# Attention with three score regions in one five-bank PSUM tile, one batch of products per group, and ScalarE's copy of turned weights ahead of the next exponential

## The chip, the core and the metric

The kernel runs on one NeuronCore of a Trainium2 chip. Its time is the device time of one launch in microseconds (us). Five engines take part, each with an instruction queue of its own that is worked through in order: TensorE (PE in the profile, with its weight loads as PEld), VectorE (DVE), ScalarE (ACT), GpSimd (POOL) and SyncE (SP, which issues transfers). They meet through semaphores. Products land in PSUM, a memory of eight banks of 512 fp32 columns on 128 partitions.

## What is computed

The reference is two transformer layers and a hybrid block (gated linear attention, an mLSTM memory and a state-space layer, then a feed-forward net). The change touches only the two attentions of the transformer layers: 512 latent and 256 context tokens of width 1024, 16 heads each. The first has 4 heads to one key/value head (GQA), and the context rows attend too; in the second each head has keys and values of its own (MLA), and only the latent rows attend.

```python
def block_attention(q, k, v):          # swept over blocks of 128 queries
    ...
    def one_block(qi):
        s = jnp.einsum('bqhgd,bkhd->bhgqk', qi, k, preferred_element_type=jnp.float32) * scale
        p = jax.nn.softmax(s, axis=-1).astype(v.dtype)
        return jnp.einsum('bhgqk,bkhe->bqhge', p, v)
```

## The kernel before, in words

Both attentions run through one routine, `attend`. Its work is a list of units. A unit is one head's 128 queries against all 768 keys (in the first attention also, for the context rows, two heads' 128 queries against 256 keys). Four heads' units, or two such pairs, make a group whose outputs are written together. The GQA attention has 64 long units in 16 groups and then 16 short units in 8 groups. The MLA attention has 64 units, four for each of 16 heads; stages of its own (projections of keys, values and queries, their rotation, and the casts of a head pair) are woven between the units at given positions.

What happens to a unit:

- `scores` (L716, MLA L1013): TensorE multiplies queries with keys into a PSUM tile `s` of 128x768 fp32. Queries and keys are split into high and low parts, so GQA has two and MLA three products for each of the two column pieces (512 and 256, a product may not cross a bank).
- the row maximum (L603, VectorE reads `s`), and `bias` (L680, MLA L997), which makes the exponent's offset from it.
- `exps` (L631, ScalarE reads `s`, writes the weights `p` to SBUF and sums them; the read of the sum is a small instruction of its own).
- `softmax_end`: the sum's reciprocal (L637, VectorE) and the scaling of `p` (L640, GpSimd).
- `turn`, LAG = 4 units later: six transposes of `p` on TensorE (L660; L653 in short units) into tiles `pt`, four in the first and two in the second, copied to SBUF as `pT` by ScalarE and VectorE (L661, L655).
- `products`, when a group's four units are turned: TensorE multiplies `pT` with the values into a PSUM tile `ob` (L722, MLA L1021), 12 products for a long group (the trace shows each as two rows). `high` casts `ob` to fp32r on ScalarE (L734, MLA L1034) and `low` takes the remainder on VectorE (L738, MLA L1040); both run in a later pass through the loop.
- `prepare`, once a group: transposes of the next queries (`tq`, L698) and their split (L702, L703, L706, L707).

Inside `manual_schedule` each engine's instructions stand in the order in which the code issues them: nothing reorders them, and the framework only adds the semaphore waits that the tiles' uses call for. So the body of the loop over `n` is the order of each queue. In one pass it issues the pending `high`s, the exponential of unit n-1, `turn` of unit n-4, the scores of unit n with their maximum and bias, `softmax_end` of unit n-1, the pending `low`s, a stage if one is due, and a few of the group's products: `per` keys, 2 in long GQA groups, 1 in short ones, 3 in MLA. A group's products are thus spread over two or three passes.

PSUM before: two tiles `s` of 1024 columns (two banks each, `pss` with bufs=2), and a pool `psp` of four tiles of one bank, from which `pt`, `tq`, the stages' `st` and `ob` are taken in turn.

Of the kernel before, what the change touches and what calls it, by code (L numbers as in the profile page):

```python
# [9 lines left out]
F32 = mybir.dt.float32  # L10
# [6 lines left out]
PSUM = bass.MemoryType.PSUM  # L17
P = 128
# [8 lines left out]
class Bump:  # L27


    def __init__(self, *regions):  # L30
        self.free = list(regions)
        self.tags = {}
# [273 lines left out]
class GqaNet(Base):  # L306
# [103 lines left out]
    def gqa(self):  # L410
        nc, i, tc, flow = self.nc, self.i, self.tc, self.flow
        W = i["gqa_w_qkv"][0]
        with ExitStack() as ph:
# [6 lines left out]
            with tc.tile_pool(name="q0", bufs=1, reuse_waits="tile") as pool, tc.tile_pool(name="q0ps", bufs=2, reuse_waits="tile", space=PSUM) as ps:  # L420
# [46 lines left out]
                b = self.turn_cols(rows, ps, pool, "b")  # L467
# [52 lines left out]
                            flow.add(ada.pop(0))  # L520
                flow.finish()
                self.ada_bufs = 2
            with tc.tile_pool(name="a0", bufs=1, reuse_waits="tile") as pool, tc.tile_pool(name="a0s", bufs=2, reuse_waits="tile", space=PSUM) as pss, \
                    tc.tile_pool(name="a0p", bufs=4, reuse_waits="tile", space=PSUM) as psp:
                units = []
                for ts in (range(4), (4, 5)):
                    for o in range(2):
                        for t in ts:
                            for g in (2 * o, 2 * o + 1):
                                gr = GqaGroup(self, pool, Q, K, V, t, g)  # L530
                                units += [(gr, (x,)) for x in range(4)] if t < 4 else [(gr, (0, 1)), (gr, (2, 3))]
                stages = {}
                none = lambda: None
                for n, (gr, xs) in enumerate(units):
                    if xs[0] == 0:
                        stages.setdefault(n - 3, []).append(gr.prepare(psp))
                n = 8
                for t in range(6):
                    for f in self.q_rope(None, Q, t, 1):
                        stages.setdefault(n, []).append((f, none, none))  # L540
                        n += 2
                ada = self.ada_steps(0, 11, pool, psp, None, True)
                next(ada)
                for x in range(2):
                    stages.setdefault(1 + x, []).insert(0, (lambda: next(ada, None), none, none))
                self.ahead = []
                for x in range(2):
                    for y, f in enumerate(self.out_weights(i["gqa_w_o"][0], x)):
                        stages.setdefault(n - 2 + 6 * x + 2 * y, []).append((f, none, none))
                self.attend(units, pool, pss, psp, stages)  # L550
# [18 lines left out]
    def attend(self, units, pool, pss, psp, stages):  # L569

        nc = self.nc
        N = len(units)
        work, highs, lows = [], [], []
        for n in sorted(k for k in stages if k < 0):
            for fs in stages[n]:
                for f in fs:
                    f()
        with self.tc.manual_schedule():  # L580
            for n in range(N + LAG + 6):
                for f in highs:
                    f()
                highs, late, lows = [], lows, []
                if 1 <= n <= N:
                    self.exps(pool, *units[n - 1])
                if LAG < n <= N + LAG and units[n - LAG - 1][0].last == units[n - LAG - 1][1][-1]:
                    g, xs = units[n - LAG - 1]
                    g.ob = psp.tile([P, 2, 128], F32, name="ob", tag="pt")
                    work.append((g, g.products()))  # L590
                if LAG <= n < N + LAG:
                    g, xs = units[n - LAG]
                    self.turn(pool, psp, g, xs)
                if n < N:
                    g, xs = units[n]
                    s = pss.tile([P, 1024], F32, name="s", tag="s")
                    m = self.sp.tile([P, 3, 2], F32, name="sm", tag="sm", bufs=6)
                    for k, x in enumerate(xs):
                        g.scores(x, s[:, k * g.nk:(k + 1) * g.nk])
                    if n == 0:  # L600

                        nc.scalar.activation(self.sp.tile([P, 1], F32, name="se", tag="se", bufs=1), s[:, :1], AF.Exp, scale=0.0)
                    nc.vector.tensor_reduce(out=m[:, 0, :len(xs)], in_=s[:, :g.nk * len(xs)]  # L603
                                            .rearrange("p (k n) -> p k n", k=len(xs)), axis=AX.X, op=ALU.max)
                    g.sm[xs] = s, m
                    g.bias(xs, m)
                if 1 <= n <= N:
                    self.softmax_end(*units[n - 1])
                for f in late:
                    f()  # L610
                for pe, high, low in stages.get(n, []):
                    pe()
                    highs.append(high)
                    lows.append(low)
                if work:
                    g, fs = work[0]
                    for f in fs[:g.per]:
                        f()
                    del fs[:g.per]
                    if not fs:  # L620
                        work.pop(0)
                        highs.append(g.high)
                        lows.append(g.low)
            assert not work and not highs and not lows

    def exps(self, pool, g, xs):
# [37 lines left out]
class GqaGroup:  # L664


    def __init__(self, net, pool, Q, K, V, t, g):
        self.net, self.pool, self.Q, self.K, self.V, self.t, self.g = net, pool, Q[t], K, V, t, g
        self.c0, self.nk = (0, NL + NC) if t < 4 else (NL, NC)
        self.keys = list(range(6)) if t < 4 else [4, 5]  # L670
        self.p, self.sm, self.last = {}, {}, 3
        self.per = 2 if t < 4 else 1

    def scale(self, x):
        return self.net.RS[:, self.t, 4 * self.g + x:4 * self.g + x + 1]
# [32 lines left out]

        return turn, high, low

    def scores(self, x, s):
        q = self.q[x % 2][:, 128 * (x // 2):128 * (x // 2) + 128]
        for j in range(2):
            for n0 in range(0, self.nk, 512):
                n1 = min(self.nk, n0 + 512)
                self.net.nc.tensor.matmul(s[:, n0:n1], lhsT=q, rhs=self.K[j][:, self.g, self.c0 + n0:self.c0 + n1],  # L716
                                          start=j == 0, stop=j == 1)

# [265 lines left out]
class MlaHead:  # L984

    last = 3
    per = 3

    def __init__(self, m, h):
        self.m, self.net, self.h, self.nk = m, m.net, h, NL + NC  # L990
# [13 lines left out]
            self.pT.append(pool.tile([P, 6, 2, 128], F32, name="pT", tag="pT", bufs=3))  # L1004
        return self.pT[x // 2][:, :, x % 2, :]

    def scores(self, x, s):
        e = self.h % 2
        (qh, ql), (kh, kl) = self.m.Q[e], self.m.K[e]
        c = slice(128 * x, 128 * x + 128)  # L1010
        for k, (a, b) in enumerate(((qh, kh), (qh, kl), (ql, kh))):
            for n0, n1 in ((0, 512), (512, 768)):
                self.net.nc.tensor.matmul(s[:, n0:n1], lhsT=a[:, c], rhs=b[:, n0:n1], start=k == 0, stop=k == 2)  # L1013

    def products(self):
# [32 lines left out]
class MlaNet(MlpNet):  # L1048
    def mla(self):
        nc, i, tc = self.nc, self.i, self.tc  # L1050
        m = Mla(self)
        self.m = m
        with ExitStack() as ph:
            mp = ph.enter_context(tc.tile_pool(name="mp", bufs=1, reuse_waits="tile"))
            tcf = [T.rearrange("p a b -> p (a b)") for T in self.TC]
            xf = self.XN.rearrange("p a b -> p (a b)")
            m.cqT = [mp.tile([P, 3, NL], F32R, name=f"cqT{j}") for j in range(2)]
            m.ckT = [t[:, :1536].rearrange("p (k n) -> p k n", k=2) for t in tcf]
            m.qpe = xf[:, :2048].rearrange("p (t h f) -> p t h f", t=4, h=16)


            kk = mp.tile([P, 2, 2, NL + NC], F32R, name="K")
            m.K = [[kk[:, e, j, :] for j in range(2)] for e in range(2)]
            m.Q = [[tcf[j][:, 1536:] for j in range(2)], [mp.tile([P, NL], F32R, name=f"Q1{j}") for j in range(2)]]
            with tc.tile_pool(name="mA", bufs=1, reuse_waits="tile") as pool:
                self.mla_in(pool, m, kk.rearrange("p e j n -> p (e j n)"))
            self.l0.close()
            with tc.tile_pool(name="a1", bufs=1, reuse_waits="tile") as pool, tc.tile_pool(name="a1s", bufs=2, reuse_waits="tile", space=PSUM) as pss, \
                    tc.tile_pool(name="a1p", bufs=4, reuse_waits="tile", space=PSUM) as psp:
                self.mla_attend(pool, pss, psp, m.cqT, m.ckT, m.qpe, m)  # L1070

    def row_rs(self, pool, x, n):
# [1625 lines left out]
```

## Time and profile before

| | |
|---|---|
| median of 3 runs | 2687.36 us (2685.77 to 2690.11) |
| the profiled execution's own time | 2689.55 us |
| its span | 2687.7 us |
| GQA attention, long units | 158.9 to 310.5 us of the span |
| GQA attention, short units | 310.5 to 348.3 us |
| MLA attention, 64 units | 1064.8 to 1292.4 us |

The page of the profile gives each engine's busy time over the span. The views of the trace used below are: a table of stretches (busy time of each engine in each), the waits (which instruction waited for which, summed), and the timeline (single instructions in order of time; "idle before" in brackets, with what ended it). Times of the timeline count from the span's start.

### The profile page before, as it was taken

What the parts mean: (1) busy time and instruction counts of PE and PEld (TensorE: products, weight loads), DVE (VectorE), ACT (ScalarE), POOL (GpSimd) and SP (SyncE); (2) the same over time, 40 slices, a digit from 0 to 9 for tenths busy, and PEclk for the clock granted to TensorE, in tenths of its full rate; (3) what the DMA queues carried; (4) which work ended last, traced back from release to release, by engine and by line L of the source; (5) the groups of instructions that cost most, each with busy time, mean ns of one, the idle gap of its engine ahead of it and who ended that gap; (6) DMA issues with size and microseconds to landing.
All of it is one profiled execution on the core that took longest, in us unless ns stands there. A gap on an engine that the chain in (4) does not pass through costs nothing. (4 is left out here: it accounts for less than half of the span.)

```text
span 2687.7 us, 37906 instructions
## 1 busy us (share of the span) xinstructions
PE 2588.1 (96%) x14954; PEld 2118.7 (79%) x14954; DVE 1734.3 (65%) x3102; ACT 1156.9 (43%) x2016; POOL 649.7 (24%) x541
## 2 busy tenths in 40 slices
PE   8999999999999999999999899989999999999998
PEld 5666689888888898777787678877678888888887
DVE  4458847876666577788488987576675533534445
ACT  4357835333333235655364344253563223532222
POOL 0224322233322013333134445043140011000000
PEclk9999999999999999999999999999999999999999
DMA  8510221333333112000255454234123234222221
GB/s 317 205 32 1 66 92 34 124 120 126 118 122 101 62 39 69 19 33 17 64 166 172 138 174 158 95 107 117 46 68 102 86 94 137 75 94 94 94 94 63
DMA packets 178644, 264.83 MB, mean 99 GB/s; under 512 B 18019, under 2 KB 116954, under 8 KB 177954
## 3 DMA queue, kind: packets, MB, share of 16 engines
q1 hardware_dynamic: 173010, 257.89, 29.0%
q10 hardware_dynamic: 5456, 4.51, 0.6%
q8 instruction: 118, 1.93, 0.3%
q14 instruction: 60, 0.49, 0.1%
HBM read 256.81 MB, written 5.58 MB: 98 GB/s over the span
## 5 line engine op out<-in xcount | busy, mean ns | idle before, releaser
L129 DVE TENSOR_TENSOR wl<-raw,wh 128x1024 fp32r<-128x1024 f32 (+1 forms) x301 | 397.7, 1334 | 358.8 <-ACT wh L126 355.9
L126 ACT CAST wh<-raw 128x1024 fp32r<-128x1024 f32 (+1 forms) x301 | 306.7, 1034 | 618.8 <-PE mm L140 449.7
L139 PE MATMUL mm<-TL,wh 128*128 128x512 f32 (+2 forms) x1512 | 565.7, 375 | 6.1 <-ACT TL L387 4.7
L140 PE MATMUL mm<-TL,wh 128*128 128x512 f32 (+2 forms) x1512 | 561.5, 372 | 4.5 <-DVE TL L388 4.4
L141 PE MATMUL mm<-TL,wl 128*128 128x512 f32 (+2 forms) x1512 | 560.1, 371 | 0.0
L139 PEld LDWEIGHTS mm<-TL,wh 128*128 128x128 f32 (+1 forms) x1512 | 287.2, 190 | 60.5 <-ACT TL L387 5.6
L140 PEld LDWEIGHTS mm<-TL,wh 128*128 128x128 f32 (+1 forms) x1512 | 287.7, 190 | 54.8 <-DVE TL L388 6.0
L141 PEld LDWEIGHTS mm<-TL,wl 128*128 128x128 f32 (+1 forms) x1512 | 287.3, 190 | 52.5
L139 PE MATMUL mm<-TC,wh 128*128 128x256 f32 (+1 forms) x672 | 223.6, 333 | 7.8 <-ACT low L867 7.8
L640 POOL TENSOR_SCALAR p<-p,sm 128x768 f32<-128x768 f32 (+1 forms) x160 | 156.1, 978 | 297.0 <-DVE sm L637 201.9
L141 PE MATMUL mm<-TC,wl 128*128 128x256 f32 (+1 forms) x672 | 223.0, 332 | 0.0
L140 PE MATMUL mm<-TC,wh 128*128 128x256 f32 (+1 forms) x672 | 222.8, 332 | 0.0
L258 POOL TENSOR_TENSOR XN<-XN 128x512 f32<-128x512 f32 x84 | 132.4, 1594 | 282.4 <-ACT XN L251 279.6
L139 PE MATMUL mm<-gh,wh 128*128 128x256 f32 (+1 forms) x544 | 179.7, 330 | 0.3 <-DVE RL L878 0.3
L140 PE MATMUL mm<-gl,wh 128*128 128x256 f32 (+1 forms) x544 | 178.7, 329 | 0.0
L141 PE MATMUL mm<-gh,wl 128*128 128x256 f32 (+1 forms) x544 | 178.1, 328 | 0.0
L258 POOL TENSOR_TENSOR low<-low 128x512 f32<-128x512 f32 x84 | 136.0, 1632 | 152.9 <-ACT low L251 150.1
L603 DVE TENSOR_REDUCE sm<-s 128x1 f32<-128x768 f32 (+1 forms) x144 | 132.7, 922 | 22.5 <-PE s L1013 11.4
L139 PEld LDWEIGHTS mm<-TC,wh 128*128 128x128 f32 x672 | 127.5, 190 | 23.3 <-ACT low L867 9.1
L140 PEld LDWEIGHTS mm<-TC,wh 128*128 128x128 f32 x672 | 127.6, 190 | 13.9
L141 PEld LDWEIGHTS mm<-TC,wl 128*128 128x128 f32 x672 | 127.6, 190 | 12.7
L660 PE MATMUL pt<-ident,p 128*128 128x128 f32 x768 | 116.0, 281 | 17.5 <-ACT pT L661 7.8
(614 smaller groups left out, 4978.8 us busy)
## 6 DMA issues: line engine op xcount, KB each, us to landing
raw<-in_mlp_w_dram SPq DMA_DIRECT2D x64, 1024.0 KB
raw<-in_w_in_dram SPq DMA_DIRECT2D x26, 1024.0 KB
XN<-in_w_ada_dram SPq DMA_DIRECT2D x24, 1024.0 KB
low<-in_ada_w_dram SPq DMA_DIRECT2D x24, 1024.0 KB
raw<-in_ffn_w_in_dram SPq DMA_DIRECT2D x22, 1024.0 KB
adaw<-in_w_ada_dram SPq DMA_DIRECT2D x21, 1024.0 KB
raw<-in_ffn_w_out_dram SPq DMA_DIRECT2D x11, 1024.0 KB
raw<-in_gqa_w_qkv_dram SPq DMA_DIRECT2D x6, 1024.0 KB
```

The lines of the kernel that those rows point to most:

```text
L126: nc.scalar.copy(h, v)
L129: nc.vector.tensor_tensor(l, v, h, op=ALU.subtract)
L139: nc.tensor.matmul(out, lhsT=ah, rhs=bh, start=start, stop=False)
L140: nc.tensor.matmul(out, lhsT=ah, rhs=bl, start=False, stop=False)
L141: nc.tensor.matmul(out, lhsT=al, rhs=bh, start=False, stop=stop)
L258: nc.gpsimd.tensor_tensor(rows[k], rows[k], rows[k + h], op=ALU.add)
L603: nc.vector.tensor_reduce(out=m[:, 0, :len(xs)], in_=s[:, :g.nk * len(xs)] .rearrange("p (k n) -> p k n", k=len(xs)), axis=AX.X, op=ALU.max)
L640: nc.gpsimd.tensor_scalar(out=g.p[xs][:, c], in0=g.p[xs][:, c], scalar1=m[:, 2, k:k + 1], scalar2=1.0, op0=ALU.mult, op1=ALU.mult)
L660: nc.tensor.transpose(tp[:, 128 * (x - lo):128 * (x - lo) + 128], p[:, 128 * x:128 * x + 128], self.ident)
```

## The change

- One tile `S` of 128x2560 fp32 (five banks) takes the place of the two tiles `s` and of `ob`. Unit n's scores go to columns 768*(n mod 3) onward: three regions. The group's output `ob` is columns 2304 to 2559. Regions 0 and 1 meet in the middle of the second bank; region 2 ends in the middle of the fifth, whose other half is `ob`.
- The pieces of the score products are cut where a region crosses a bank (512+256, or 256+512 for region 1).
- `psp` has three tiles in place of four.
- `per` is gone: all products of a group are issued in one pass.
- `turn(n-4)` is issued ahead of `exps(n-1)`: on ScalarE the copy of turned weights now stands before the exponential. On TensorE this changes nothing, since an exponential issues nothing there.

```diff
-  pss bufs=2, psp bufs=4
+  pss bufs=1, psp bufs=3        (both attentions)
 def attend(...):
+    S = pss.tile([P, 2560], F32, name="s", tag="s")
     ...
                 highs, late, lows = [], lows, []
-                if 1 <= n <= N:
-                    self.exps(pool, *units[n - 1])
                 if LAG < n <= N + LAG and ...:
                     g, xs = units[n - LAG - 1]
-                    g.ob = psp.tile([P, 2, 128], F32, name="ob", tag="pt")
+                    g.ob = S[:, 2304:].rearrange("p (a n) -> p a n", a=2)
                     work.append((g, g.products()))
                 if LAG <= n < N + LAG:
                     g, xs = units[n - LAG]
                     self.turn(pool, psp, g, xs)
+                if 1 <= n <= N:
+                    self.exps(pool, *units[n - 1])
                 if n < N:
                     g, xs = units[n]
-                    s = pss.tile([P, 1024], F32, name="s", tag="s")
+                    c0 = 768 * (n % 3)
+                    s = S[:, c0:c0 + 768]
                     ...
                     for k, x in enumerate(xs):
-                        g.scores(x, s[:, k * g.nk:(k + 1) * g.nk])
+                        a, b = c0 + k * g.nk, c0 + (k + 1) * g.nk
+                        cut = min(b, (a // 512 + 1) * 512)
+                        g.scores(x, s[:, k * g.nk:(k + 1) * g.nk], [(p - a, q - a) for p, q in ((a, cut), (cut, b)) if q > p])
                 ...
                 if work:
-                    g, fs = work[0]
-                    for f in fs[:g.per]:
+                    g, fs = work.pop(0)
+                    for f in fs:
                         f()
-                    del fs[:g.per]
-                    if not fs:
-                        work.pop(0)
-                        highs.append(g.high)
-                        lows.append(g.low)
+                    highs.append(g.high)
+                    lows.append(g.low)
```

In the rows of the order, an engine's queue is listed with the source line, the operation, output<-inputs by the program's names and the shape; "waits" names the engines' semaphores that the instruction waits on, and x3 counts alike neighbours. `s` is the score tile (after the change the whole of `S`, `ob` included), `pt` the transposes' tile, `K` and `q` keys and queries.

TensorE, a stretch of two passes in the middle of the long GQA units, before:

```order
L722 MATMUL ob<-pT,V 64x256 x4
L660 MATMUL pt<-ident,p 128x128 [waits DVE_49,Pool_49]
L660 MATMUL pt<-ident,p 128x128 x3
L660 MATMUL pt<-ident,p 128x128 [waits Activation_49]
L660 MATMUL pt<-ident,p 128x128
L716 MATMUL s<-K_86,q_1871 128x512
L716 MATMUL s<-K_86,q_1871 128x256
L716 MATMUL s<-K_87,q_1871 128x512
L716 MATMUL s<-K_87,q_1871 128x256
```

The same place after the change, a pass with a group's products and the scores on both sides of it:

```order
L718 MATMUL s<-K_86,q_1626 128x256 [waits Activation_49]
L718 MATMUL s<-K_86,q_1626 128x512
L718 MATMUL s<-K_87,q_1626 128x256
L718 MATMUL s<-K_87,q_1626 128x512
L724 MATMUL s<-pT,V 64x256 [waits DVE_49]
L724 MATMUL s<-pT,V 64x256 x11
L664 MATMUL pt<-ident,p 128x128 [waits PE_49,Pool_49]
L664 MATMUL pt<-ident,p 128x128 x3
L664 MATMUL pt<-ident,p 128x128 [waits PE_49]
L664 MATMUL pt<-ident,p 128x128
L718 MATMUL s<-K_86,q_1627 128x512 [waits Activation_49]
```

The products stand in one batch of 12 and write the tile named `s`; the first of them waits for VectorE, and the first product of each unit's scores waits for ScalarE.

ScalarE, the end of a group in the same stretch, before:

```order
L631 ACTIVATE p,sm<-s,sm,RS 128x768 [waits DVE_49,Pool_49]
L661 COPY pT<-pt 128x4x128 [waits PE_49]
L734 CAST TL_75<-ob 128x2x128 [waits PE_49]
L631 ACTIVATE p,sm<-s,sm,RS 128x768 [waits DVE_49,Pool_49]
L661 COPY pT<-pt 128x4x128 [waits PE_49]
L631 ACTIVATE p,sm<-s,sm,RS 128x768 [waits DVE_49,PE_49,Pool_49]
```

After:

```order
L665 COPY pT<-pt 128x4x128 [waits PE_49,Activation_49]
L635 ACTIVATE p,sm<-s,sm,RS 128x768 [waits DVE_49,Pool_49]
L736 CAST TL_75<-s 128x2x128 [waits DVE_49,PE_49]
L665 COPY pT<-pt 128x4x128 [waits PE_49]
L635 ACTIVATE p,sm<-s,sm,RS 128x768 [waits DVE_49,Pool_49]
```

Between the cast of the group's output and the exponential there now stands the copy of turned weights, and the cast waits for VectorE as well as for TensorE.

## Rows read from the trace of the kernel before

**Rows 1.** The page, busy time of each engine (share of the span, instructions).

```profile
PE 2588.1 (96%) x14954; PEld 2118.7 (79%) x14954; DVE 1734.3 (65%) x3102; ACT 1156.9 (43%) x2016; POOL 649.7 (24%) x541
```

**Rows 2.** Stretches: long and short GQA units, the 64 MLA units.

```profile
core 0: us, PE busy (x) PEld busy (x) DVE busy (x) ACT busy (x) POOL busy (x), PEclk, DMA share, GB/s
158.90:310.50 151.60, 145.38 (x1013) 101.94 (x1013) 132.42 (x331) 118.39 (x247) 67.45 (x68) 1.00 0.12 40
310.50:348.30 37.80, 36.85 (x273) 24.29 (x270) 31.29 (x88) 32.02 (x100) 16.71 (x34) 1.00 0.17 56
1064.80:1292.40 227.60, 213.04 (x1450) 165.86 (x1449) 183.68 (x382) 133.11 (x285) 79.70 (x63) 0.99 0.08 25
```

**Rows 3.** Waits, long GQA units (160 to 310 us): total, times, longest.

```profile
ACT p L631 <- DVE sm L637: 28.8, 29, 2.2
PE s L716 <- ACT p L631: 2.3, 3, 0.9
```

**Rows 4.** Timeline of long GQA units: start, duration, engine, instruction.

```profile
227.18 0.95 PE L716 MATMUL s<-K,q 128*128 128x512 f32 x4
...
228.24 0.96 DVE L603 TENSOR_REDUCE sm<-s 128x1 f32<-128x768 f32 x1 [0.35 <-PE s L716]
...
229.07 0.87 PE L660 MATMUL pt<-ident,p 128*128 128x128 f32 x6
229.19 0.37 ACT L734 CAST TL<-ob 128x256 fp32r<-128x256 f32 x1 [0.36 <-PE ob L722]
...
229.71 0.95 PE L716 MATMUL s<-K,q 128*128 128x512 f32 x4
...
230.47 0.57 ACT L661 COPY pT<-pt 128x512 f32<-128x512 f32 x1
...
232.43 0.16 DVE L680 SCALAR_TENSOR_TENSOR sm<-sm,RS 128x1 f32<-128x1 f32 x1
232.58 0.40 DVE L738 TENSOR_TENSOR TL<-ob,TL 128x256 fp32r<-128x256 f32 x1
232.71 0.99 ACT L631 ACTIVATE p<-s,sm,RS 128x768 f32<-128x768 f32 x1 [1.67 <-DVE sm L637]
```

**Rows 5.** Timeline of MLA units, three places (1134, 1271 and 1116 us).

```profile
1134.26 1.29 PE L1013 MATMUL s<-K,Q 128*128 128x512 f32 x6
...
1135.48 1.53 PE L1205 MATMUL st<-ident,XN 128*32 128x128 f32 x16
1135.66 0.96 DVE L603 TENSOR_REDUCE sm<-s 128x1 f32<-128x768 f32 x1 [0.69 <-PE s L1013]
1136.65 0.15 DVE L997 TENSOR_SCALAR sm<-sm 128x1 f32<-128x1 f32 x1
...
1271.40 0.91 ACT L631 ACTIVATE p<-s,sm 128x768 f32<-128x768 f32 x1 [4.82 <-DVE sm L637]
...
1272.44 1.31 PE L1013 MATMUL s<-K,TC 128*128 128x512 f32 x6 [0.28 <-ACT p L631]
...
1275.24 0.75 ACT L1034 CAST TL<-ob 64x256 fp32r<-64x256 f32 x2
...
1116.16 0.93 DVE L1323 TENSOR_TENSOR K<-kt,K 64x768 fp32r<-64x768 f32 x1
...
1118.86 0.85 DVE L1040 TENSOR_TENSOR TL<-ob,TL 64x256 fp32r<-64x256 f32 x2
```

**Rows 6.** Timeline, the last group of the MLA attention: its 24 product rows.

```profile
1300.31 2.93 PE L1021 MATMUL ob<-pT,V 128*64 128x256 f32 x24
```

**Rows 7.** Stretches, for TensorE's granted clock (the column PEclk).

```profile
1085.00:1087.00 2.00, 0.55 (x4) 0.31 (x4) 1.97 (x5) 1.05 (x3) 1.00 (x1) 1.00 0.73 269
1087.30:1090.70 3.40, 3.23 (x12) 2.95 (x13) 3.32 (x8) 0.57 (x3) 0.86 (x2) 0.51 0.02 5
1275.00:1283.00 8.00, 5.00 (x33) 3.81 (x31) 7.81 (x16) 3.53 (x9) 3.74 (x4) 1.00 0.40 131
```

**Rows 8.** Timeline, the same score products at half clock.

```profile
1087.81 2.27 PE L1013 MATMUL s<-K,TC 128*128 128x512 f32 x6
```

More of the change, by code (lines that the diff above doesn't have):

```diff
@@ L522, in gqa @@
                 self.ada_bufs = 2
-            with tc.tile_pool(name="a0", bufs=1, reuse_waits="tile") as pool, tc.tile_pool(name="a0s", bufs=2, reuse_waits="tile", space=PSUM) as pss, \
-                    tc.tile_pool(name="a0p", bufs=4, reuse_waits="tile", space=PSUM) as psp:
+            with tc.tile_pool(name="a0", bufs=1, reuse_waits="tile") as pool, tc.tile_pool(name="a0s", bufs=1, reuse_waits="tile", space=PSUM) as pss, \
+                    tc.tile_pool(name="a0p", bufs=3, reuse_waits="tile", space=PSUM) as psp:
                 units = []
@@ L671, in __init__ @@
         self.p, self.sm, self.last = {}, {}, 3
-        self.per = 2 if t < 4 else 1
     def scale(self, x):
@@ L709, in prepare, with scores @@
         return turn, high, low
-    def scores(self, x, s):
+    def scores(self, x, s, cuts):
         q = self.q[x % 2][:, 128 * (x // 2):128 * (x // 2) + 128]
         for j in range(2):
-            for n0 in range(0, self.nk, 512):
-                n1 = min(self.nk, n0 + 512)
+            for n0, n1 in cuts:
                 self.net.nc.tensor.matmul(s[:, n0:n1], lhsT=q, rhs=self.K[j][:, self.g, self.c0 + n0:self.c0 + n1],
@@ L986 @@
     last = 3
-    per = 3
     def __init__(self, m, h):
@@ L1005, in turned, with scores @@
         return self.pT[x // 2][:, :, x % 2, :]
-    def scores(self, x, s):
+    def scores(self, x, s, cuts):
         e = self.h % 2
@@ L1011, in scores @@
         for k, (a, b) in enumerate(((qh, kh), (qh, kl), (ql, kh))):
-            for n0, n1 in ((0, 512), (512, 768)):
+            for n0, n1 in cuts:
                 self.net.nc.tensor.matmul(s[:, n0:n1], lhsT=a[:, c], rhs=b[:, n0:n1], start=k == 0, stop=k == 2)
@@ L1067, in mla @@
             self.l0.close()
-            with tc.tile_pool(name="a1", bufs=1, reuse_waits="tile") as pool, tc.tile_pool(name="a1s", bufs=2, reuse_waits="tile", space=PSUM) as pss, \
-                    tc.tile_pool(name="a1p", bufs=4, reuse_waits="tile", space=PSUM) as psp:
+            with tc.tile_pool(name="a1", bufs=1, reuse_waits="tile") as pool, tc.tile_pool(name="a1s", bufs=1, reuse_waits="tile", space=PSUM) as pss, \
+                    tc.tile_pool(name="a1p", bufs=3, reuse_waits="tile", space=PSUM) as psp:
                 self.mla_attend(pool, pss, psp, m.cqT, m.ckT, m.qpe, m)
```

## The prediction

> **What bounds the kernel now.** I read the page first, then the stretches of the two attentions, then their waits, then single units on the timeline. TensorE is busy 96% of the span [rows 1], and in the attentions too: 145.4 of 151.6 us in the long GQA units, 36.9 of 37.8 in the short, 213.0 of 227.6 in MLA [rows 2]. So a unit is paced by TensorE: 151.6/64 = 2.37 us in GQA, 227.6/64 = 3.56 in MLA. A unit's own softmax is longer than its pace, but it is off the path: with two score tiles TensorE does other units' scores, transposes and products in the meantime. The waits show it: ScalarE waits 28.8 us for maxima and biases in 150 us, and TensorE waits for an exponential only 2.3 [rows 3]. What can be won by removing every TensorE gap is 6.2 + 1.0 + 14.6 = 22 us [rows 2].
>
> **What the change does to the order.** The idea of three regions is that unit n's scores need only unit n-3's exponential. In the built program it is otherwise. Waits belong to tiles, and there is now one tile. The first score product of each unit waits on ScalarE for the count that the *previous* unit's exponential reaches, whichever region either of them uses; the order shows that wait on each unit's scores, where before one unit in several carries one. The maximum waits for it too, the products (which write the same tile) wait for the maximum of their own pass, the cast of the group's output waits for that maximum and the last product, and the exponential after a remainder (`low`) waits for that. Scores, maximum, bias, exponential and the next scores become one chain, with one unit in it. That "three regions" act as less than one buffer is my main case.
>
> **A plain unit of that chain.** GQA: scores start to maximum 228.24 - 227.18 = 1.06; maximum to bias 0.99 (1136.65 - 1135.66 in MLA, the same shape); bias to exponential 232.71 - 232.43 = 0.28; exponential to next scores 1.04 in MLA (1272.44 - 1271.40) and 0.08 more here for 0.99 instead of 0.91 us of work, 1.12. Sum 3.45 against a pace of 2.37. MLA: scores to maximum 1135.66 - 1134.26 = 1.40, then 0.99 + 0.28 + 1.04: 3.71 against 3.56 [rows 4, 5]. Transposes and scaling lie beside this and cost nothing while it is the longest chain: from the scores, TensorE's transposes (0.64, 229.71 - 229.07), ScalarE's copy (0.57) and the exponential give a little less.
>
> **A unit with a batch.** No batch of a GQA group stands in this trace; the nearest row is the last MLA group, 24 rows in 2.9 us [rows 6]. GQA: the maximum ends 1.06 + 0.96 after the scores begin, 2.1 with a signal; products to 5.0; transposes, now behind them, to 5.6; the copy, now ahead of the exponential, starts a tenth later and takes 0.57, to 6.3; exponential to next scores 1.12: 7.4. The cast (0.12 after the products, 0.37) is done by 5.5. Here both other edits bite: the exponential could have started at 2.3, but stands behind a cast and a copy that wait for the batch. The unit after it has the remainder (0.40) ahead of the exponential: 3.85. A group is 7.4 + 3.85 + 2 x 3.45 = 18.15. Of 16 groups the batches of 14 fall in the long stretch: 14 x 18.15 + 8 x 3.45 = 282, **+130**. The short units have the same chain; I price them by the same ratio (estimate), 282/151.6 x 37.8 = 70, **+32**.
>
> **MLA, per block of eight units.** Eight plain units 29.7. Two batches: 2.4 to the end of the maximum, 5.3 after the products, casts (0.12 + 0.75) to 6.2, copy to 6.75, exponential 1.04: 7.8, 4.1 over a plain unit, 8.2 for both. Stages on TensorE: 213.0/64 = 3.33 a unit, less scores 1.22 (1135.48 - 1134.26), transposes 0.64 and products 2.9/4, leaves 0.74, 5.9 a block; 1.2 of it lies in a batch's wait for its maximum and 0.6 in the slack of the copy chain (3.57 against 3.71), 4.1 stay. Casts of a head pair: the remainders of the group's output stand behind 1116.16 to 1119.71 on VectorE (1118.86 + 0.85), 3.55 us of casts' remainders and their own, and the exponential waits for them; in the other half block 0.85. Sum 46.4 a block; seven such, a first one without batches (35), less 4 for the stages that the last lacks: 356 against 227.6, **+128** [rows 2, 5, 6].
>
> The sum is 290 at full clock. The cuts at banks change no count of products and cost nothing; one `pt` tile fewer is covered by the new idle time, and costs nothing as long as the chain is longer than transposes and copies. Against the profiled execution's 2689.6 this gives 2980. The median lies 2 us lower, which I leave inside the range.
>
> **The clock.** A plain GQA unit would keep TensorE busy 0.95 + 0.87 of 3.45 us. In the trace the granted clock fell to half after 1085 to 1087 (0.55 of 2 us busy), and six score products took 2.27 us, not 1.29; it stayed full from 1275 to 1283 with 5.0 of 8 us busy [rows 5, 7, 8]. The new units lie between the two. Price: 2.27/1.29 is 0.75 more for TensorE's work on the chain, that is 4 x 1.06 + 2.9 + 0.64 = 7.8 a GQA group and 8 x 1.40 + 2 x 3.54 + 4.1 = 22.4 an MLA block; 14 x 5.8 + 8 x 0.8 + 8 x 16.8 and a quarter of the first two for the short units: 244 us if the clock were at half throughout. Nothing excludes either end, 0 or 244. I take a third, 81, since the long idle times after batches and casts resemble the first row and plain units rather the second: 3060.
>
> By the Trainium skill ("TensorE: Matmul & The Clock Gate", Part 4, PE-mode transpose) transposes don't count as busy for the clock as matmuls do; then only 0.95 of 3.45 us would count, and the high end would hold. The stretch at 1275 to 1283 speaks against it in part: transposes are among its 5.0 us, and the clock stayed full.
>
> **Rivals.**
> - *The clock stays full* (like 1275 to 1283): 2980. It decides if gaps of 1.5 us never lower it.
> - *Half clock through both attentions*: 2980 + 244 = 3224.
> - *Waits go by bank.* Only region 1 after region 0 meets in a bank, so one unit in three is serial: 21 x 1.08 + 21 x 0.15 = 26, a few for the short ones, and some 20 for batches that meet region 2 in the fifth bank: 2740. Against it: the order shows a wait at every unit. The Trainium skill ("PSUM — Partial Sum Buffer", PSUM bank collisions raise a hardware error) asks for semaphores by bank, since two engines in one bank collide, reads included. That rule would leave two units in three free; the program's waits are stricter than it, and no row of before can show that.
> - *Faster: the regions act as three buffers.* If the awaited exponential lay two units back or more, a turn of 3.45/2 = 1.73 is below the pace of 2.37 in GQA (MLA 1.86 against 3.56), TensorE paces again, its gaps of 22 us close, and batches save a few switches: 2665. That point, one unit back or two, decides; the built program says one.
> - *No change*: gaps and waits cancel, 2689.
>
> **How the numbers follow.** Main case 0.55 (3060), full clock 0.26 (2980), half clock 0.13 (3224), by bank 0.02, faster 0.03, no change 0.01. For the first two the clock's share runs from none to two thirds (2980 + 163 = 3143), and the sizes of the chain, of which MLA's stages are the least sure, by some 40 more at the upper end and 30 at the lower: 2950 to 3190, which leaves out under 0.2. A measurement here can tell 0.2% from no change; faster by more 0.03, within 0.01, slower by more 0.96.
>
> **What would show it.** In the profile after, the first score product of nearly every unit should have a wait for ScalarE's exponential, and GQA units should stand 3.4 to 3.6 us apart, 7 to 8 where a batch is; a GQA stretch of some 280 us, MLA 350 to 360, more with PEclk below 1. TensorE's gaps should sum to some 250 us and more, not 22. Outside the attentions nothing should move. I am wrong if scores start before the previous exponential has ended, or if a batch doesn't delay the exponential behind it; and in size if PEclk is 1.00 or 0.5 throughout.

## The result and the profile after

The changed kernel takes 3047.39 us (median of 4 runs, 3044.14 to 3053.22) against 2686.57 (2684.05 to 2690.11): a ratio of 1.1342, 95% interval 1.1326 to 1.1358, 361 us slower. Predicted were 3060, within 2950 to 3190.

The page after, its busy line and two rows of the span in 40 slices (tenths of busy time, tenths of full clock):

```profile
PE 2673.9 (88%) x14954; PEld 2171.3 (71%) x14954; DVE 1741.5 (57%) x3102; ACT 1172.0 (38%) x2016; POOL 649.9 (21%) x541
...
PE   8965566999999999866666998999998999999999
...
PEclk9989986999999999999898999999999999999999
```

The instructions are as many as before [rows 1]; TensorE's share falls from 96% to 88%, in two places of the span; elsewhere its slices read 8 or 9. The stretches of the two attentions, from first scores to last products, after:

```profile
core 0: us, PE busy (x) PEld busy (x) DVE busy (x) ACT busy (x) POOL busy (x), PEclk, DMA share, GB/s
160.30:463.30 303.00, 176.06 (x1013) 121.69 (x1012) 138.62 (x335) 128.66 (x250) 69.57 (x69) 0.89 0.06 20
463.30:552.20 88.90, 58.29 (x271) 38.17 (x271) 30.94 (x84) 32.42 (x97) 15.83 (x33) 0.64 0.13 42
1266.00:1662.20 396.20, 256.35 (x1522) 194.12 (x1520) 191.50 (x402) 143.69 (x298) 81.12 (x67) 0.90 0.06 17
```

MLA with its tail before:

```profile
1065.00:1303.20 238.20, 222.34 (x1520) 172.15 (x1518) 189.56 (x396) 138.34 (x296) 82.42 (x66) 0.99 0.09 28
```

Long GQA units went from 151.6 to 303, short ones from 37.8 to 89 [rows 2], and MLA with its tail from 238 to 396: together some 360 us, the whole loss. Two things make it up. TensorE's gaps were 6 + 1 + 16 = 23 us and are 127 + 31 + 140 = 297: 274 more. And for the same instructions TensorE was busy 491 us instead of 404, since its clock was granted at 0.64 to 0.90: 86 more, part of it beside the chain, where it costs nothing.

Where the gaps end is told by the waits of the long GQA units after (the first row) and of MLA (the two others): total, times, longest.

```profile
PE s L718 <- ACT p L635: 110.0, 63, 2.6
```

```profile
PE s L1014 <- ACT p L635: 130.1, 63, 5.5
...
ACT p L635 <- DVE TL L1041: 32.0, 14, 4.0
```

Of 64 units, 63 wait for an exponential before their scores, 110 and 130 us, where before three waits in 150 us made 2.3 [rows 3]. Two plain GQA units and one with a batch on the timeline after:

```profile
206.20 0.97 PE L718 MATMUL s<-K,q 128*128 128x256 f32 x4 [2.01 <-ACT p L635]
...
207.27 0.96 DVE L609 TENSOR_REDUCE sm<-s 128x1 f32<-128x768 f32 x1 [1.97 <-PE s L718]
...
208.26 0.16 DVE L683 SCALAR_TENSOR_TENSOR sm<-sm,RS 128x1 f32<-128x1 f32 x1
...
208.52 0.99 ACT L635 ACTIVATE p<-s,sm,RS 128x768 f32<-128x768 f32 x1 [0.29 <-DVE sm L641]
...
209.65 0.97 PE L718 MATMUL s<-K,q 128*128 128x512 f32 x4 [1.83 <-ACT p L635]
...
213.11 0.97 PE L718 MATMUL s<-K,q 128*128 128x512 f32 x4 [1.83 <-ACT p L635]
214.19 0.96 DVE L609 TENSOR_REDUCE sm<-s 128x1 f32<-128x768 f32 x1 [1.92 <-PE s L718]
215.19 0.16 DVE L683 SCALAR_TENSOR_TENSOR sm<-sm,RS 128x1 f32<-128x1 f32 x1
215.21 2.81 PE L724 MATMUL s<-pT,V 128*64 128x256 f32 x24 [1.12 <-DVE sm L609]
...
217.95 0.87 PE L664 MATMUL pt<-ident,p 128*128 128x128 f32 x6
218.06 0.37 ACT L736 CAST TL<-s 128x256 fp32r<-128x256 f32 x1 [5.00 <-PE s L724]
218.64 0.59 ACT L665 COPY pT<-pt 128x512 f32<-128x512 f32 x1 [0.20 <-PE pt L664]
...
219.12 1.00 ACT L635 ACTIVATE p<-s,sm,RS 128x768 f32<-128x768 f32 x1
...
220.26 0.96 PE L718 MATMUL s<-K,q 128*128 128x256 f32 x4 [1.44 <-ACT p L635]
```

Read it as a chain: scores, 1.07 later the maximum, 0.99 later the bias, 0.26 later the exponential, 1.13 later the next scores. That is 3.45 us for the first unit, and 3.46 for the second. In the third unit the products start when the maximum has ended (215.21), and the transposes behind them start at 217.95. The bias was ready at 215.35, but the exponential starts at 219.12, behind a cast and a copy that wait for the batch. This unit takes 7.15 us.

### The profile page after: what moved, and what is told of

The parts are those of the page before. It is cut to its first block, busy times and chain, and to the rows that moved or that the text cites. A ratio compares the mean times of both kernels' runs of the same rounds, so it can differ in the third digit from the quotient of the medians.

```text
span 3045.1 us, 38004 instructions
## 1 busy us (share of the span) xinstructions
PE 2673.9 (88%) x14954; PEld 2171.3 (71%) x14954; DVE 1741.5 (57%) x3102; ACT 1172.0 (38%) x2016; POOL 649.9 (21%) x541
## 5 line engine op out<-in xcount | busy, mean ns | idle before, releaser
L718 PE MATMUL s<-K,q 128*128 128x256 f32 (+1 forms) x320 | 84.1, 392 | 133.1 <-ACT p L635 131.5
L718 PEld LDWEIGHTS s<-K,q 128*128 128x128 f32 x320 | 54.4, 217 | 158.3 <-ACT p L635 153.3
```

## Experiments

Times are medians; each ratio is to the kernel before, run beside the experiment on the same chip (2686 to 2687 us).

**Separate tiles.** The changed kernel with scores in two tiles and the output in a third:

```diff
-        S = pss.tile([P, 2560], F32, name="s", tag="s")
-                    g.ob = S[:, 2304:].rearrange("p (a n) -> p a n", a=2)
+                    g.ob = pss.tile([P, 512], F32, name="ob", tag="ob", bufs=1)[:, :256].rearrange("p (a n) -> p a n", a=2)
-                    c0 = 768 * (n % 3)
-                    s = S[:, c0:c0 + 768]
+                    c0 = 0
+                    s = pss.tile([P, 1024], F32, name="s", tag="s", bufs=2)
```

> The changed kernel, but scores in two separate two-bank tiles and the group's output in a tile of its own; batch, three pt tiles and ScalarE's order stay. Theory (the waits of one tile made the chain of one unit at a time): the loss of 361 us goes nearly whole, 2680 to 2740 us; GQA units about 2.4 us apart, MLA about 3.6. Rival (the batch and the copy ahead of the exponential cost it by themselves): at least half of the loss stays, 2860 us or more.

Measured 2689.59 us, ratio 1.0014 (1.0005 to 1.0024). All but 3 of the 361 us are gone, with the batch and ScalarE's order kept. TensorE's wait for exponentials, 160 to 310 us of that kernel:

```profile
PE s L717 <- ACT p L634: 2.3, 4, 0.9
```

It is the 2.3 us of the kernel before. Two score tiles thus undo the loss while the batch, the order and three `pt` tiles stay.

**One tile alone.** The reverse: the kernel before, products spread and order kept, with all scores in one tile of regions and three `pt` tiles, from which the output is taken too.

```diff
...
+        S = pss.tile([P, 2560], F32, name="s", tag="s")
-                    s = pss.tile([P, 1024], F32, name="s", tag="s")
+                    c0 = 768 * (n % 3)
+                    s = S[:, c0:c0 + 768]
...
-  psp bufs=4
+  psp bufs=3
```

> The kernel before with one change: all scores in three regions of one five-bank tile (three pt tiles; the group's output stays among these). Products spread over passes and ScalarE's order as before. Theory: the chain alone, GQA units at 3.45 us instead of 2.37 (64 x 1.08 = 69 us more, short units some 20, MLA 50 to 70), clock full, since the spread products fill the gaps: 2810 to 2860 us. Rival (batch and order are the cost): within 10 us of 2687.

Measured 2861.53 us, ratio 1.0654 (1.0638 to 1.067): 175 us slower, just above the upper edge. The timeline of that kernel:

```profile
206.85 0.97 PE L722 MATMUL s<-K,q 128*128 128x512 f32 x4 [1.85 <-ACT p L638]
207.75 1.08 PE L728 MATMUL ob<-pT,V 128*64 128x256 f32 x8
...
210.33 0.98 PE L722 MATMUL s<-K,q 128*128 128x256 f32 x4 [0.69 <-ACT p L638]
```

Units stand 3.48 us apart with spread products in the gap. From the first maximum of the long GQA units (160.88) to the first of the short ones (399.61) it is 238.7 us, against 151.4 before. But it isn't the chain alone. TensorE's waits from 158 to 400 us:

```profile
PE s L722 <- ACT p L638: 46.0, 32, 2.6
PE pt L667 <- ACT pT L668: 16.0, 14, 1.1
```

Only half of the long units wait for an exponential. With the waits for VectorE's split of queries (9.4 us), transposes wait some 25 us for one of the three `pt` tiles, which the output shares here, and units with such a wait stand 4.1 us apart. The clock was not full either: 0.94 in this stretch, 0.982 in the mean. So one tile of scores, with one `pt` tile fewer, makes 175 of the 361 us; how the 175 divide was not tested apart.

**Batch alone, order alone.** Each in the kernel before:

```diff
-                    for f in fs[:g.per]:
+                    for f in fs:
```

> The kernel before with one change: all products of a group in one pass. Theory: two score tiles cover the 2.9 us, and TensorE has the same work: 2675 to 2720 us. Rival (a batch by itself delays the exponentials behind it by 3.7 to 5.4 us each, 40 batches): 2840 us or more.

Measured 2697.72 us, ratio 1.0043 (1.0028 to 1.0058).

```diff
-                if 1 <= n <= N:
-                    self.exps(pool, *units[n - 1])
                 if LAG <= n < N + LAG:
                     g, xs = units[n - LAG]
                     self.turn(pool, psp, g, xs)
+                if 1 <= n <= N:
+                    self.exps(pool, *units[n - 1])
```

> The kernel before with one change: ScalarE's copy of turned weights ahead of the next exponential. Theory: scores wait for the exponential two units back, so a delay of the exponential by one copy (0.57) and its transposes is covered most of the time: 2680 to 2730 us. Rival (order by itself serialises): 2800 us or more.

Measured 2693.26 us, ratio 1.0025 (1.0016 to 1.0035). Where two units are under way, a batch costs 11 us and the copy ahead of the exponential 7. Both rivals fall. That the batch's 2.8 us cost so much more in the changed kernel goes with the one tile, since separate tiles take the cost away with the batch in place.

**The output apart, the old order.** Two parts of the changed kernel undone, one by one:

```diff
-                    g.ob = S[:, 2304:].rearrange("p (a n) -> p a n", a=2)
+                    g.ob = psp.tile([P, 2, 128], F32, name="ob", tag="pt")
```

> The changed kernel, but the group's output in a pt tile and not in the score tile; batch and ScalarE's order stay. Theory: the batch no longer waits for the maximum of its pass (about 1 us in each of 48 passes) and the remainder no longer holds the next exponential (0.4 to 0.85): 40 to 90 us less, 2960 to 3005 us. Rival (the output's place costs nothing; the score waits alone do it): 3035 us or more.

Measured 2935.68 us, ratio 1.0932 (1.0916 to 1.0948): 112 us back, more than either theory gave. Units with a GQA batch take 5.96 us instead of 7.15 at full clock. In MLA the 64 maxima span 333 us instead of 382. What changed there is seen in a unit with a head pair's casts. The changed kernel, then the one with the output apart:

```profile
1314.97 0.15 DVE L998 TENSOR_SCALAR sm<-sm 128x1 f32<-128x1 f32 x1
1315.22 0.95 DVE L1324 TENSOR_TENSOR K<-kt,K 64x768 fp32r<-64x768 f32 x1
...
1318.02 0.85 DVE L1041 TENSOR_TENSOR TL<-s,TL 64x256 fp32r<-64x256 f32 x2
1318.97 0.90 ACT L635 ACTIVATE p<-s,sm 128x768 f32<-128x768 f32 x1 [3.28 <-DVE TL L1041]
...
1320.02 2.29 PE L1014 MATMUL s<-K,TC 128*128 128x256 f32 x6 [4.79 <-ACT p L635]
```

```profile
1301.20 0.15 DVE L998 TENSOR_SCALAR sm<-sm 128x1 f32<-128x1 f32 x1
1301.45 0.90 ACT L635 ACTIVATE p<-s,sm 128x768 f32<-128x768 f32 x1 [0.23 <-DVE sm L641]
...
1302.49 1.34 PE L1014 MATMUL s<-K,TC 128*128 128x512 f32 x6 [1.74 <-ACT p L635]
```

In the first the exponential waits for the remainder (L1041), which stands behind the head pair's casts on VectorE: 4.0 us from bias to exponential, TensorE idle 4.79, and the next scores at half clock (2.29 instead of 1.3). With the output apart the exponential starts 0.25 us after the bias. My expectation counted the remainder's own 0.4 to 0.85 and forgot what it stands behind, though the prediction had priced that. It also left out the clock, whose mean rose from 0.959 to 0.978.

The old order in the changed kernel:

```diff
+                if 1 <= n <= N:
+                    self.exps(pool, *units[n - 1])
                 if LAG < n <= N + LAG and ...:
                 ...
                     self.turn(pool, psp, g, xs)
-                if 1 <= n <= N:
-                    self.exps(pool, *units[n - 1])
```

> The changed kernel, but ScalarE's exponential ahead of the copy of turned weights, as before. Theory: in a pass with a batch the exponential still stands behind the cast of the output, which ends at about 5.4 us where the copy ended at 6.2: 0.7 us less in 48 batches, 20 to 40 us: 3005 to 3027 us. Rival (the order is the main part of what the batch costs in the chain, 186 us over the one-tile kernel): 2900 us or less.

Measured 3040.39 us, ratio 1.1318 (1.1301 to 1.1335): 7 us, less than expected and not clear of noise, since its interval overlaps that of the changed kernel (1.1326 to 1.1358). The mean clock fell from 0.959 to 0.940. A stretch of that kernel, a plain unit and one with a batch:

```profile
207.26 1.65 PE L718 MATMUL s<-K,q 128*128 128x512 f32 x4 [1.23 <-ACT p L635]
...
211.42 1.65 PE L718 MATMUL s<-K,q 128*128 128x512 f32 x4 [1.23 <-ACT p L635]
...
218.80 0.37 ACT L736 CAST TL<-s 128x256 fp32r<-128x256 f32 x1 [6.95 <-PE s L724]
219.07 1.00 ACT L635 ACTIVATE p<-s,sm,RS 128x768 f32<-128x768 f32 x1
```

The exponential now follows the cast at once, and where the clock was full a batch unit took 6.37 us, 0.8 less than 7.15. But here scores take 1.65 us: plain units run 4.16 us apart at half clock. Only 2 of the 14 long GQA batches took 6.37; the other 12 took 8.05 to 8.50. From first to last maximum the long GQA units took 308 us, 9 more than in the changed kernel, and MLA 367, 15 less. So in the GQA units the lower clock took more than the order gave.

**The clock.** Extra score products into an unread tile keep TensorE busy while it waits (this adds work and leaves the output as it was):

```diff
+                    if n >= 4:
+                        ft = psp.tile([P, 512], F32, name="pt", tag="pt")
+                        for k in range(2 if g.nk > 512 else 4):
+                            g.scores(xs[0], ft, [(0, min(g.nk, 512))])
```

> The changed kernel with extra score products in every pass ahead of unit n's own, written to a pt tile that nobody reads, so that TensorE works while it waits for the exponential (it adds work and leaves the output as it was). Theory (part of the loss is the granted clock, which falls in those waits): mean clock from 0.959 to 0.98 or more, units at 7.14 where the batch took 8.84, and the time 30 to 70 us below the changed kernel's 3047: 2980 to 3017 us. Rival (the clock costs nothing that matters, the chain is bound by other engines): 3047 us or more, since work was added.

Measured 3014.06 us, ratio 1.1221 (1.1202 to 1.1239), mean clock 0.978: 33 us faster than the changed kernel, with more work. Plain units (3.45) and batches at full clock (7.14) take as long as without the filler; batches at half clock fell from 9 to 7 of the 14 long ones. From the clocks, (1 - 0.959) x 2 x 3045 = 250 us were at half in the changed kernel and 132 here: 0.28 us of time for each us at half. By that the 210 us of half clock in its attentions (from the three stretches, 2 x 303 x 0.11 and so on) cost about 59 us. This is an estimate, and a low one if the filler itself costs anything, which is in the 33.

**Tiles that meet at a bank's edge.** The changed kernel's five banks as two tiles:

```diff
-        S = pss.tile([P, 2560], F32, name="s", tag="s")
+        SA = pss.tile([P, 1536], F32, name="sA", tag="sA")
+        SB = pss.tile([P, 1024], F32, name="sB", tag="sB")
-                    g.ob = S[:, 2304:].rearrange("p (a n) -> p a n", a=2)
+                    g.ob = SB[:, 768:].rearrange("p (a n) -> p a n", a=2)
-                    c0 = 768 * (n % 3)
-                    s = S[:, c0:c0 + 768]
+                    c0 = (0, 768, 0)[n % 3]
+                    s = (SA, SA, SB)[n % 3][:, c0:c0 + 768]
```

> The changed kernel in the same five banks at the same columns, but as two tiles that meet at a bank's edge: regions 0 and 1 in one of three banks, region 2 and the group's output in one of two. Theory (a wait per tile): only region 1 after region 0 is serial, a third of the one-tile cost of 175 us is 58, and batches still collide with region 2: 2720 to 2800 us, so 250 to 330 us of the loss go. Rival (three regions or five banks cost it in another way): above 2900 us.

Measured 2859.84 us, ratio 1.0649 (1.0633 to 1.0665): half the loss goes, where I expected seven tenths or more. To see why, the same split made in the one-tile kernel (products spread, the old order, the output in a `pt` tile):

```diff
-        S = pss.tile([P, 2560], F32, name="s", tag="s")
-                    s = S[:, c0:c0 + 768]
+        SA = pss.tile([P, 1536], F32, name="sA", tag="sA")
+        SB = pss.tile([P, 1024], F32, name="sB", tag="sB")
+                    s = (SA, SA, SB)[n % 3][:, c0:c0 + 768]
```

> The kernel with all scores in one tile (e2, 175 us slower than before), but as two tiles that meet at a bank's edge; products spread, ScalarE's order as before, the group's output in a pt tile. Theory (a wait per tile, and in the bank-tiles run the batch behind it kept the rest): one unit in three is serial, a third of 175 is 58: 2735 to 2765 us. Rival (each serial unit costs more than its share, since ScalarE's queue then runs late for the next ones): 2790 us or more.

Measured 2789.89 us, ratio 1.0384 (1.0368 to 1.04): 103 us, at the rival's edge. TensorE's waits in that kernel, 158 to 1500 us:

```profile
PE sA L1020 <- ACT p L639: 23.6, 19, 3.4
PE sA L723 <- ACT p L639: 21.6, 18, 2.6
PE pt L668 <- ACT pT L669: 19.0, 21, 1.1
PE pt L668 <- DVE q L715: 10.3, 16, 0.7
```

The tile `sA`, which holds two regions, stalls scores 37 times in 144 units, 1.2 us each time; another 29 us are transposes that wait for a `pt` tile, of which there is one fewer than before. These waits name 74 of the 103 us. That a serial unit delays ScalarE's and VectorE's copies, and these the next transposes, fits; it wasn't tested apart.

**Three real buffers.** Six banks in three tiles, two banks for all else; the rest as in the changed kernel:

```diff
-                    s = S[:, c0:c0 + 768]
+                    s = pss.tile([P, 1024], F32, name="s", tag="s", bufs=3)
-  psp bufs=3
+  psp bufs=2        (the group's output among them)
```

> The changed kernel with what three regions were to give, in three separate two-bank tiles (six banks), and the two banks left for transposes, stages and the group's output in turn; batch and ScalarE's order stay. Theory (TensorE hardly waits for exponentials with two score tiles, 2.3 us in 150, so a third has little to give; two pt tiles make transposes wait for their copies): 2690 to 2760 us. Rival (a third buffer closes TensorE's gaps of 22 us): 2675 us or less.

Measured 2851.05 us, ratio 1.0619 (1.0604 to 1.0634). Far over either expectation: the mechanism was as expected, the size was not. Its waits, 158 to 1500 us:

```profile
PE pt L663 <- ACT pT L664: 61.2, 84, 1.3
...
PE pt L663 <- DVE TL L739: 22.8, 15, 1.6
```

No score waits for an exponential any more, but the second transposes of a unit wait for the copy before them, 84 times, and others wait for the output's remainder. The two rows make 84.0 us of the 165. The clock has a part as well: in the long GQA units, 158 to 408 us, it was granted at 0.76, and TensorE was busy 192 us instead of 145. The banks that three score buffers need are worth more as `pt` tiles.

**The output's own tile.** In the kernel before, first with spread products, then with the batch:

```diff
-                    g.ob = psp.tile([P, 2, 128], F32, name="ob", tag="pt")
+                    g.ob = pss.tile([P, 512], F32, name="ob", tag="ob", bufs=1)[:, :256].rearrange("p (a n) -> p a n", a=2)
...
-  psp bufs=4
+  psp bufs=3
```

> The kernel before with the group's output in a one-bank tile of its own and three pt tiles in place of four; products spread, order as before. The two-tile run is 4 us slower than before where the batch alone costs 11 and the order alone 7: either the own tile gives some 10 us back (then 2674 to 2682 us here), or the two costs overlap and the tile gives nothing (2684 to 2692 us).

> The same with the batch of products (so the two-tile run but with ScalarE's exponential ahead of the copy). If the order costs 7 us here as it does alone: 2680 to 2685 us. If the copy ahead of the exponential helps where a batch is issued (pt tiles come free sooner): 2692 us or more.

Measured 2712.01 us, 1.0092 (1.0078 to 1.0106), and 2703.04 us, 1.0067 (1.0054 to 1.0079). The first is outside both expectations, the second on the side of the copy's help. The own tile gives nothing back; with spread products it costs 25 us, of which TensorE's waits name 23 (158 to 1400 us):

```profile
PE ob L722 <- DVE TL L738: 12.3, 14, 1.7
...
PE ob L722 <- DVE TC L738: 10.7, 7, 2.4
```

The one output tile is not free when the next group's products start. The second of these kernels is the separate-tiles kernel with the old order: 2703 against 2690. The copy ahead of the exponential, 7 us dear alone, gives 13 back there. TensorE's largest waits for a `pt` tile (158 to 1400 us), old order first, then the copy ahead:

```profile
PE pt L659 <- ACT pT L660: 20.0, 33, 1.9
PE pt L659 <- DVE pT L660: 11.1, 22, 1.3
```

```profile
PE pt L663 <- ACT pT L664: 5.5, 15, 0.6
```

All of them together are 33 and 16 us. So ScalarE's new order frees `pt` tiles sooner, which is worth something where units overlap and these tiles are few. No version beat the kernel before; the best, 2689.59, is within 0.2% of it.

## Why the prediction was right, step by step

- *One chain, one unit in it.* Right: 63 of 64 units wait, separate tiles take the loss away, and one tile of scores with three `pt` tiles brings half of it. That the lost `pt` tile costs nothing holds for the changed kernel, where no wait for one is among TensorE's in the long GQA units; in the one-tile run, with the output in these tiles, it does not.
- *Plain unit 3.45, after a remainder 3.85, with a batch 7.4 (GQA).* Measured 3.45, 3.84 to 3.86, and 7.15 at full clock; the products were taken at 2.9 and took 2.74 to the next transposes.
- *+130 for the long GQA units, +32 for the short, at full clock.* Measured 151.4 and 51 with the clock at 0.89 and 0.64. The price of the short ones was the long units' ratio and no sum of rows.
- *MLA block 46.4, +128 in all.* After the first block the blocks' maxima stand 48.2 to 52.5 us apart, with the clock at 0.90, and MLA with its tail took 158 us more. The remainder held behind a head pair's casts, predicted 3.55, showed as 4.0 from bias to exponential instead of the usual 0.25.
- *The sum at full clock, 290, and the clock 81.* By the filler run the clock's part is some 59 us. The unit lengths say more: the 56 long GQA units from the first batch on took 269.5 us, where units at full clock add up to 251. That is 19 us for the 49 at half there (clock 0.91), 0.39 for each, and 0.39 x 210 is 82. Both are estimates. With the clock at 59 to 82 the chain makes 279 to 302, and both terms of the prediction lie within; closer than that no run tells them apart. The third of the half-clock price was the weaker step: two rows stood for the two ends and nothing fixed the place between them, so that 3060 came so near 3047 is in part luck. The attentions were at half for 210 of 788 us; 27% of the full price of 244 would have been 65.
- *TensorE's gaps "some 250 us and more".* 297.
- *The clock's pattern.* The text held that idle time after batches and casts lowers the clock. What stood out is the batch itself:

```profile
233.11 4.49 PE L724 MATMUL s<-pT,V 128*64 128x256 f32 x24 [1.12 <-DVE sm L609]
```

```profile
206.20:213.10 6.90, 3.25 (x20) 2.56 (x20) 4.75 (x12) 3.34 (x6) 1.81 (x2) 1.00 0.00 0
...
233.00:237.00 4.00, 3.89 (x20) 2.23 (x22) 1.38 (x5) 0.00 (x0) 2.55 (x2) 0.57 0.02 4
```

Most plain units kept the clock full (1.00 with 3.25 of 6.9 us busy); it had fallen by the time a batch began, in 9 of the 14 long GQA batches, whose units then took 8.8 us instead of 7.15, and came back within the unit. The places named for the fall were only partly right.
- *The rivals.* "Half clock through both attentions" and "the clock stays full" both fall, with 0.89 to 0.90 in the long stretches and 0.64 in the short. The rule on transposes that the prediction cites for the half-clock case is not borne out in the plain units above, which were granted 1.00 with scores and transposes alone on TensorE; no run here tries transposes by themselves. Of "waits go by bank" the experiment shows that the mechanism exists where tiles are cut at banks, but its price of some 50 us was too low: 103 with spread products and 174 with the batch. The Trainium skill ("PSUM — Partial Sum Buffer", PSUM bank collisions raise a hardware error) asks for guards by bank. No run here tried a guard by address, which that page rules out. Cut at the bank's edge, the three regions of 768 columns leave one pair in a shared tile, and that pair, with one `pt` tile fewer, kept 103 of the 175 us.

## What to carry to other kernels

A buffer is what the waits treat as one: regions of one tile are one buffer, however far apart their columns lie, and readers of it wait for each other too. Before cutting a tile into regions, look at which instruction each first write waits for in the built order, and multiply the serial chain by the number of units. And where two buffers already hide the softmax, count what the banks for a third are taken from: here three score tiles with two `pt` tiles took 2851 us, two with three `pt` tiles and a bank for the output 2690.

## What I had not expected of the hardware

The same work ran for several us at either clock level. In the changed kernel plain GQA units ran 3.45 us apart at a granted clock of 1.00; in the old-order run such units ran 4.16 us apart at 0.50. The first row below holds a plain unit and the start of one with a batch, the second its products, the third what follows:

```profile
207.20:214.20 7.00, 4.59 (x16) 3.39 (x16) 3.60 (x9) 2.04 (x5) 0.91 (x1) 0.50 0.00 0
214.20:218.70 4.50, 4.50 (x25) 2.45 (x25) 0.79 (x3) 0.00 (x0) 1.20 (x1) 0.60 0.00 0
218.70:224.00 5.30, 2.70 (x20) 2.10 (x18) 2.27 (x6) 3.63 (x9) 0.91 (x1) 1.00 0.00 0
```

TensorE was busy 66% of the first stretch at half clock, as against 47% of the plain units' at full, and the clock came back in the 4.5 us of products behind it. Why it fell in one kernel and not in the other is not shown. So a gain of 0.8 us a batch was lost to the clock in the GQA units, and the filler, which only adds work, made the kernel 33 us faster.
